# Sparse expert blocks brought back inside the last chunk, with their transfers on Pool's queue

## The chip, the core and the metric

The kernel runs on one core of a Trainium2 chip. The metric is the device time of one execution in microseconds. TensorE (PE in the profile) does matmuls, VectorE (DVE) and ScalarE (ACT) elementwise work, GpSimd (POOL) some of it and DMA issues, SyncE (SP) DMA issues. Each engine takes its instructions in the order in which they stand on its own queue, and waits on semaphores for the others.

## What is computed

One layer of a decoder: attention beside a state-space mixer, and then the PEER expert network, in which each token chooses 128 of 16384 experts (8 heads of 16). Only the second half matters here:

```python
    def block(args):
        hb, ib, gb = args
        u = jnp.take(u_experts, ib, axis=0)
        pre = jnp.einsum('thkd,td->thk', u, hb).astype(jnp.float32)
        act = (jax.nn.gelu(pre, approximate=False) * gb).astype(hb.dtype)
        vsel = jnp.take(v_experts, ib, axis=0)
        return jnp.einsum('thk,thkd->td', act, vsel)
...
        x = x + g2 * peer_ffn(h2, w_query[l], sub_keys[l], u_experts[l], v_experts[l])
```

512 tokens with 2048 features; the output is the residual stream after both halves.

## The kernel before

**Two ways for the experts.** Of the 512 tokens, 160 are *sparse*: their experts' rows are gathered one by one. The other 352 (TD) are *dense*: all 16384 experts are computed for them, and a matrix of gates, zero for the experts not chosen, picks. The dense part is the large one on TensorE, the sparse part lies beside it on VectorE and Pool.

**The dense loop** goes over 16 chunks of 8 expert blocks (`for c in range(P // CH)`). In a chunk, `up` makes eight blocks of activations (matmuls "up"), VectorE multiplies them with the gates gc, and they are split in a high and a low part, ah and al. Then four passes over dg follow, each for four of the 16 groups of 128 features: 96 matmuls "pv" (8 blocks, 4 features, 3 products of the split parts) fill four PSUM accumulators pv0 to pv3, and four VectorE instructions x1s add them to the residual stream (x1s <- pv, modT, x1s). In the last chunk each x1s is followed by a store of its 128 features of the dense tokens, issued on SP.

**Weights** come by SP in pieces of 512 KB (ur, vr), ScalarE rounds them to a high part (uh, vh), and VectorE makes the low part (ul, vl, line 131). These splits have to be ready ahead of TensorE.

**The sparse part** is a list of 320 entries, for each of 160 slots one u row and one v row per partition: Pool gathers 1 MB (`pick`, line 1080) into one of three buffers g. A u entry (line 1086) multiplies with the tokens and sums; a v entry (line 1098) adds a row times its coefficient to an accumulator with tokens on the partitions: acc0 for the first 128 slots (128 tokens), accx for the last 32 (32 tokens, four partitions to a token). `step()`, called 16 times a chunk, issues and consumes the entries; consumption is held two entries behind (AHEAD).

**The end.** After the loops the remaining entries are consumed, and each accumulator is brought back to features. ACT issues the load of the tokens' residual stream xb. TensorE turns the accumulator (lines 1178 and 1180): for acc0 16 transposes, for accx 16 matmuls with the stationary accx and the moving matrix `fold`, which also sums the four partitions of a token. VectorE adds the result to xb (line 1183), and SP issues the store. xb takes a buffer of the same three as g; the results "op" and the accumulators pv share 8 PSUM banks (`vps`).

**Order.** The program is written in the order of the loops, but a scheduler with a timeline model of its own puts the instructions of each engine into their final order; what stands on a queue is then fixed.

Of the kernel before, what the change touches and what calls it, by code (L numbers as in the profile page):

```python
# [11 lines left out]
F32 = mybir.dt.float32  # L12
# [5 lines left out]
ALU = mybir.AluOpType  # L18
# [4 lines left out]
P = 128  # L23
T = 512
D = 2048
KD = D // P
NT = T // P
EPS = 1e-6
CH = 8
# [3 lines left out]
NS = 160  # L33
XT = NS - P
XQ = P // XT
# [15 lines left out]
def layer(ctx, tc, xT, cols_d, pos_d, w_ada, w_in, w_kr, w_uq, w_ukv, w_out, w_q, subk, u_t, u_r, v_t, v_d, out):  # L51
    nc = tc.nc
# [49 lines left out]
    ident = cp.tile([P, P], F32, name="ident")  # L102
# [21 lines left out]
    SH1, SC1, G1, SH2, SC2, G2 = range(6)  # L124

    def mod(m, k):
        return modT[:, m * 16 + k:m * 16 + k + 1]
# [196 lines left out]
    for q in range(4):  # L324
        ada_pe(SC1, q)
        ada_pe(SH1, q, page_a)
        for k in range(4 * q, 4 * q + 4):
            hk = tp("hk")
            nc.scalar.activation(hk, xs[k], AF.Identity, scale=mod(SC1, k), bias=mod(SH1, k))
            a = [page_a("hh", F32R), page_a("hl", F32R)]  # L330
# [8 lines left out]
    for i in range(6):  # L339
        t = page_b("lat")  # L340
# [3 lines left out]
    ps = psum("pjk")  # L344
# [5 lines left out]
    ps = psum2("kdp")  # L350
# [100 lines left out]
    for n in (11, 9, 7, 5, 3, 1):  # L451
# [7 lines left out]
                                   op1=ALU.mult)  # L459
    cs = ep.tile([P, 64], F32, name="cs")  # L460
    ncs = ep.tile([P, 64], F32, name="ncs")
    ps = psum2("csp")
# [3 lines left out]
    ps = psum2("csl")  # L466
# [319 lines left out]
    x1 = []  # L786
    s2 = Sq("s2", nc.vector)
    for d in range(KD):
        t = page_b("x1")[:, :T]
        nc.sync.dma_start(t, x1d[d])  # L790
        ps = psum("wob")
# [274 lines left out]
    def gath(name):  # L1066
        return pe_.tile([P, D], F32, tag="gath", name=name, bufs=3)
# [45 lines left out]
    def step():  # L1113
        nonlocal issued, done, unit
        unit += 1
        goal = max(0, min(total, total * (unit - LAG) // (units * 15 // 16 - LAG)))
        while done < goal - AHEAD:
            f, s, _ = sparse[done]
            with tc.issue_after(pace[1].ins):
                f(s, fetched[done])  # L1120
            fetched[done] = None
            done += 1
        while issued < goal:
            f, s, table = sparse[issued]
            fetched.append(pick(s, table, "g"))
            issued += 1

    for c in range(P // CH):
        A = []
        for jj in range(CH):  # L1130
            j = c * CH + jj
            if j % GC == 0:
                gc = pe_.tile([P, NTG, GC, 32], F32, tag="gc", name="gc", bufs=1)
                nc.sync.dma_start(gc.rearrange("p g j t -> p g (j t)"), gd[j // GC])
            ge = ges.pop(j) if j in ges else up(j)
            g3 = ge.rearrange("p (g t) -> p g t", t=32)
            nc.vector.tensor_tensor(g3, g3, gc[:, :, j % GC, :], ALU.mult)
            a = [pp.tile([P, TD], F32R, tag=t, name=t) for t in ("ah", "al")]
            nc.scalar.activation(a[0], ge, AF.Copy)
            pace[1] = sub_lo(nc.vector, a[1], ge, a[0])  # L1140
            A.append(a)
            step()
        if c == 0:
            nc.gpsimd.dma_start(x1[:, CH:], x1d[CH:, :, NS:].rearrange("k p t -> p k t"))
        for dg in range(4):
            pv = [vps.tile([P, T], F32, tag="v", name=f"pv{i}") for i in range(4)]
            for j2 in range(CH // 2):
                vw = wload(v_d[c, dg, j2], (2, T), eng=nc.vector, name="v")
                pace[1] = pace[0]
                for q in range(2):  # L1150
                    jj = j2 * 2 + q
                    for dd in range(4):
                        mm(pv[dd][:, :TD], [w[:, q, dd * P:(dd + 1) * P] for w in vw], A[jj], jj == 0, jj == CH - 1)
                if j2 % 2:
                    step()
            for dd in range(4):
                d = dg * 4 + dd
                nc.vector.scalar_tensor_tensor(x1[:, d], pv[dd][:, :TD], mod(G2, d), x1[:, d], op0=ALU.mult, op1=ALU.add)
                if c == P // CH - 1:
                    nc.sync.dma_start(out[d][:, NS:], x1[:, d])  # L1160
    AHEAD = 0
    while done < total:
        step()

    fold = pe_.tile([P, XT], F32, name="fold", bufs=1)
    nc.vector.tensor_tensor(fold, ident[:, 0:XT], ident[:, XT:2 * XT], ALU.add)
    for q in range(2, XQ):
        nc.vector.tensor_tensor(fold, fold, ident[:, q * XT:(q + 1) * XT], ALU.add)
    for acc, t0, n in ((acc0, 0, P), (accx, P, XT)):
        xb = gath("xb")[:, :KD * n].rearrange("p (k t) -> p k t", k=KD)  # L1170
        nc.scalar.dma_start(xb, x1d[:, :, t0:t0 + n].rearrange("k p t -> p k t"))
        for q in range(4):
            ps = vps.tile([P, T], F32, tag="v", name="op")
            for j in range(4):
                d = q * 4 + j
                a, o = acc[:, d * P:(d + 1) * P], ps[:, j * P:j * P + n]
                if n == P:
                    nc.tensor.transpose(o, a, ident)
                else:
                    nc.tensor.matmul(o, a, fold, start=True, stop=True)  # L1180
            for j in range(4):
                d = q * 4 + j
                nc.vector.scalar_tensor_tensor(xb[:, d], ps[:, j * P:j * P + n], mod(G2, d), xb[:, d], op0=ALU.mult,
                                               op1=ALU.add)
        nc.sync.dma_start(out[:, :, t0:t0 + n].rearrange("k p t -> p k t"), xb)


def arrange(x, c, positions, w_ada, b_ada, w_in, q_a_norm, w_uq, kv_a_norm, w_ukv, q_norm, k_norm, attn_out_norm,
# [60 lines left out]
```

## Time and profile before

| | us |
|---|---|
| median of 3 runs | 3236.68 |
| lowest, highest run | 3230.98, 3237.19 |
| profiled execution, its time | 3230.25 |
| profiled execution, its span | 3228.5 |
| TensorE busy | 3063.2 (95%) |
| VectorE busy | 2488.2 (77%) |
| GpSimd busy | 941.4 (29%) |

The span goes from the first to the last instruction; the time has 1.75 us more around it. Busy time is the union of an engine's instructions, so an engine that is busy for a whole stretch sets that stretch's length, and one that is not may still be waited for at one place in it.

### The profile page before, as it was taken

The page shows a single profiled execution, that of the slowest core. Times are in us where ns is not written, and L with a number is a line of the kernel's source. Part 1 is how long each engine was busy: PE and PEld are TensorE (multiplying, and loading weights), DVE is VectorE, ACT ScalarE, POOL GpSimd, SP SyncE. Part 2 cuts the span into 40 slices and gives each one's busy share as a digit, 9 for nine tenths or more (in the row PEclk, how much of TensorE's full clock was granted, in tenths as well). Part 3 has the DMA queues.
Part 4 walks back from the last instruction along what each step waited for, and adds up shares of the span by engine and source line. Part 5 has one row for each costly group of instructions (what it writes and reads, how often), then busy time and mean ns, then how long its engine had stood idle before and what let it go on. Part 6 is the DMA issues. An engine that isn't in the chain of part 4 may idle for free.

```text
span 3228.5 us, 46353 instructions
## 1 busy us (share of the span) xinstructions
PE 3063.2 (95%) x17881; PEld 2794.6 (87%) x17881; DVE 2488.2 (77%) x3904; ACT 1146.5 (36%) x1754; POOL 941.4 (29%) x650
## 2 busy tenths in 40 slices
PE   5998889889989889999999999999999999999999
PEld 2476766567767788999999999999999999999999
DVE  3247777577759997659888888888888888888887
ACT  2243225442262257733333333333332333332332
POOL 1143333014435566533221121122222222121211
PEclk9999999999999999999999999999999999999999
DMA  9626762429642247769998999899998999999997
GB/s 320 243 93 217 235 212 95 135 99 311 230 136 76 84 125 209 232 216 369 341 343 331 338 342 330 336 341 332 336 336 331 341 338 334 340 336 336 336 343 260
DMA packets 286189, 858.79 MB, mean 266 GB/s; under 512 B 35888, under 2 KB 95424, under 8 KB 245008
## 3 DMA queue, kind: packets, MB, share of 16 engines
q1 hardware_dynamic: 181648, 483.53, 42.7%
q0 software_dynamic: 46448, 337.01, 28.0%
q10 hardware_dynamic: 57872, 35.30, 3.7%
q8 instruction: 140, 2.29, 0.3%
q14 instruction: 81, 0.66, 0.1%
HBM read 816.65 MB, written 39.06 MB: 265 GB/s over the span
## 4 chain that ended last, share of the span: by engine, by line
PE 61%; DVE 5%; ACT 2%; DMA 1%; issue 1%; POOL 1%; ACTq 0%; SPq 0%; POOLq 0%; DVEq 0%
PE pv L138 10%; PE pv L137 10%; PE pv L136 10%; PE up L136 9%; PE up L138 9%; PE up L137 9%; PE gps L1022 1%; ACT gt L1025 1%; DVE oj L1020 1%; DMA h2f<-h2b 0%; DMA sk<-subk 0%; PE wq L137 0%; PE wq L136 0%; DVE topi L933 0%; DVE topi L930 0%
## 5 line engine op out<-in xcount | busy, mean ns | idle before, releaser
L138 PE MATMUL up<-h2hi,ul 128*128 128x352 f32 x2048 | 664.2, 324 | 0.3 <-POOL ul L131 0.3
L136 PE MATMUL up<-h2hi,uh 128*128 128x352 f32 x2048 | 663.1, 324 | 0.0
L137 PE MATMUL up<-h2lo,uh 128*128 128x352 f32 x2048 | 661.2, 323 | 0.0
L136 PE MATMUL pv<-ah,vh 128*128 128x352 f32 x2048 | 659.3, 322 | 1.4 <-ACT ge L964 1.4
L137 PE MATMUL pv<-al,vh 128*128 128x352 f32 x2048 | 659.2, 322 | 0.0
L138 PE MATMUL pv<-ah,vl 128*128 128x352 f32 x2048 | 651.0, 322 | 0.0
L156 ACT ACTIVATE vh<-vr 128x1024 fp32r<-128x1024 f32 x256 | 272.1, 1063 | 624.8 <-PE pv L137 528.3
L156 ACT ACTIVATE uh<-ur 128x1024 fp32r<-128x1024 f32 x256 | 271.3, 1060 | 541.0 <-PE up L137 405.0
L131 DVE TENSOR_TENSOR vl<-vr,vh 128x1024 fp32r<-128x1024 f32 x256 | 312.6, 1223 | 157.4 <-ACT vh L156 157.1
L131 POOL TENSOR_TENSOR wl<-wr,wh 128x1024 fp32r<-128x1024 f32 (+2 forms) x134 | 294.7, 2204 | 465.8 <-ACT wh L156 377.4
L138 PEld LDWEIGHTS up<-h2hi,ul 128*128 128x128 f32 x2048 | 389.1, 190 | 0.7 <-POOL ul L131 0.7
L136 PEld LDWEIGHTS pv<-ah,vh 128*128 128x128 f32 x2048 | 384.6, 188 | 1.7 <-ACT ge L964 1.7
L137 PEld LDWEIGHTS up<-h2lo,uh 128*128 128x128 f32 x2048 | 385.9, 188 | 0.0
L136 PEld LDWEIGHTS up<-h2hi,uh 128*128 128x128 f32 x2048 | 385.8, 188 | 0.0
L137 PEld LDWEIGHTS pv<-al,vh 128*128 128x128 f32 x2048 | 384.6, 188 | 0.0
L138 PEld LDWEIGHTS pv<-ah,vl 128*128 128x128 f32 x2048 | 382.9, 188 | 0.0
L131 DVE TENSOR_TENSOR ul<-ur,uh 128x1024 fp32r<-128x1024 f32 x214 | 261.8, 1223 | 130.8 <-ACT uh L156 130.8
L1080 POOL DMA_INDIRECT g<-u_r,idx x128 | 163.2, 1275 | 576.3 <-DVE acc L1098 485.6
L1080 POOL DMA_INDIRECT g<-v_t,idx x128 | 155.7, 1217 | 541.1 <-DVE pre L1086 526.1
L1098 DVE SCALAR_TENSOR_TENSOR acc<-g,cf,acc 128x2048 f32<-128x2048 f32 x127 | 297.6, 2343 | 0.0
L1086 DVE CUSTOM_DVE_ANT_0 g<-g,h2t 128x2048 f32<-128x2048 f32 x128 | 292.0, 2283 | 2.1 <-DMA g<-u_r,idx 2.1
L269 DVE SCALAR_TENSOR_TENSOR acc<-wada,ca,acc 128x512 f32<-128x512 f32 x180 | 200.6, 1114 | 74.7 <-DMA wada<-w_ada 71.7
(465 smaller groups left out, 4786.8 us busy)
## 6 DMA issues: line engine op xcount, KB each, us to landing
ur<-u_t SPq DMA_DIRECT2D x256, 512.0 KB
vr<-v_d SPq DMA_DIRECT2D x256, 512.0 KB
wada<-w_ada SPq DMA_DIRECT2D x96, 512.0 KB
wada<-w_ada SPq DMA_DIRECT2D x128, 256.0 KB
gd<-gt ACTq DMA_DIRECT2D x22, 1024.0 KB
gc<-gd SPq DMA_DIRECT2D x32, 704.0 KB
wr<-w_in SPq DMA_DIRECT2D x40, 512.0 KB
wadq<-w_ada SPq DMA_DIRECT2D x32, 512.0 KB
```

Source lines behind the costliest of these rows:

```text
L131: return eng.tensor_tensor(lo, src, hi.bitcast(F32), ALU.subtract)
L136: nc.tensor.matmul(ps, a[0], b[0], start=start, stop=False)
L137: nc.tensor.matmul(ps, a[0], b[1], start=False, stop=False)
L138: pace[5] = nc.tensor.matmul(ps, a[1], b[0], start=False, stop=stop)
L156: nc.scalar.activation(hi[:, :n], raw[:, :n], AF.Copy)
L269: nc.vector.scalar_tensor_tensor(acc, wt[:, kk], ca[:, k:k + 1], acc, op0=ALU.mult, op1=ALU.add)
L1020: nc.vector.tensor_scalar(oj[:, t], iota, ijg[:, 1, t0 + t:t0 + t + 1], ijg[:, 2, t0 + t:t0 + t + 1], op0=ALU.is_equal, op1=ALU.mult)
L1022: pace[2] = nc.tensor.matmul(ps[:, t * P:(t + 1) * P], oi[:, t], oj[:, t], start=True, stop=True)
L1025: nc.scalar.activation(gt[:, :, t4_ * 4:t4_ * 4 + 4].rearrange("p j t -> p t j"), pv_[:, :, jh * 64:(jh + 1) * 64], AF.Copy)
L1080: nc.gpsimd.indirect_dma_start(out=g, out_offset=None, in_=table, in_offset=bass.IndirectOffsetOnAxis(ap=ix[:, s - s0:s - s0 + 1], axis=0))
L1086: nc.vector.tensor_tensor_reduce(g, g, rows, 1.0, 0.0, ALU.mult, ALU.add, accum_out=pre[:, s:s + 1])
L1098: nc.vector.scalar_tensor_tensor(acc, g, cf[:, s:s + 1], acc, op0=ALU.mult, op1=ALU.add)
```

## The change

The block that brings an accumulator back becomes a function `back`. It is called inside the last chunk: for acc0 behind the stores of the first pass (dg 0), for accx behind those of the second (dg 1). The load of xb and the store of the result are issued from Pool's queue (ACT and SP before), and so are the 16 stores of the dense tokens (SP before). When all gathers are issued, `step` consumes what is left at once, without the lag of two entries; the loop that did this behind the chunks is gone. `fold` is written ahead of the loop.

```diff
@@ step()
+        while issued == total and done < total:
+            f, s, _ = sparse[done]
+            f(s, fetched[done])
+            done += 1
+
+    fold = pe_.tile([P, XT], F32, name="fold", bufs=1)
...
+    def back(acc, t0, n):
+
+        xb = gath("xb")[:, :KD * n].rearrange("p (k t) -> p k t", k=KD)
+        nc.gpsimd.dma_start(xb, x1d[:, :, t0:t0 + n].rearrange("k p t -> p k t"))
+        for q in range(4):
+            ps = vps.tile([P, T], F32, tag="v", name="op")
+            for j in range(4):
+                d = q * 4 + j
+                a, o = acc[:, d * P:(d + 1) * P], ps[:, j * P:j * P + n]
+                if n == P:
+                    nc.tensor.transpose(o, a, ident)
+                else:
+                    nc.tensor.matmul(o, a, fold, start=True, stop=True)
+            for j in range(4):
+                d = q * 4 + j
+                nc.vector.scalar_tensor_tensor(xb[:, d], ps[:, j * P:j * P + n], mod(G2, d), xb[:, d], op0=ALU.mult,
+                                               op1=ALU.add)
+        nc.gpsimd.dma_start(out[:, :, t0:t0 + n].rearrange("k p t -> p k t"), xb)
...
                 if c == P // CH - 1:
-                    nc.sync.dma_start(out[d][:, NS:], x1[:, d])
-    AHEAD = 0
-    while done < total:
-        step()
-
-    fold = pe_.tile([P, XT], F32, name="fold", bufs=1)
...
-    for acc, t0, n in ((acc0, 0, P), (accx, P, XT)):
...
-        nc.scalar.dma_start(xb, x1d[:, :, t0:t0 + n].rearrange("k p t -> p k t"))
...
-        nc.sync.dma_start(out[:, :, t0:t0 + n].rearrange("k p t -> p k t"), xb)
+                    nc.gpsimd.dma_start(out[d][:, NS:], x1[:, d])
+            if c == P // CH - 1 and dg in (0, 1):
+                assert done == total
+                back(*((accx, P, XT) if dg else (acc0, 0, P)))
```

**TensorE's queue at the end of the program, before.** Behind the last pv matmul of the last pass stand the 16 transposes of acc0 and the 16 matmuls of accx with fold (the numbers name buffers):

```order
L137 MATMUL pv3_28662<-al_28260,vh_28755 128x352
L138 MATMUL pv3_28662<-ah_28259,vl_28756 128x352
L1178 MATMUL op_28799<-ident_83,acc0_9412 128x128 x4
L1178 MATMUL op_28808<-ident_83,acc0_9412 128x128 x4
L1178 MATMUL op_28817<-ident_83,acc0_9412 128x128 x4
L1178 MATMUL op_28826<-ident_83,acc0_9412 128x128 x4
L1180 MATMUL op_28838<-fold_28793,accx_9414 128x32 x4
L1180 MATMUL op_28847<-fold_28793,accx_9414 128x32 x4
```

TensorE's queue at the end of the second pass of the last chunk, after (pv3_28443 is the last accumulator of this pass, pv0_28611 the first of the third):

```order
L136 MATMUL pv3_28443<-ah_28265,vh_28536 128x352
L137 MATMUL pv3_28443<-al_28266,vh_28536 128x352
L138 MATMUL pv3_28443<-ah_28265,vl_28537 128x352
L1149 MATMUL op_28574<-fold_12266,accx_9414 128x32 x4
L1149 MATMUL op_28583<-fold_12266,accx_9414 128x32 x4
L1149 MATMUL op_28592<-fold_12266,accx_9414 128x32 x4
L1149 MATMUL op_28601<-fold_12266,accx_9414 128x32 x4
L136 MATMUL pv0_28611<-ah_27794,vh_28617 128x352
L137 MATMUL pv0_28611<-al_27795,vh_28617 128x352
L138 MATMUL pv0_28611<-ah_27794,vl_28618 128x352
```

The 16 matmuls that read accx moved from the end of the queue to a place ahead of the third pass; acc0's transposes likewise stand between the first and the second pass.

**VectorE's queue at the end of the program, before** (accx lines are additions of gathered rows, vl the weight splits, x1s and xb the additions to the residual stream):

```order
L131 TENSOR_TENSOR vl_28666<-vr_28663,vh_28665 128x1024
L1098 SCALAR_TENSOR_TENSOR accx_9414<-g_27651,cf_12265,accx_9414 128x2048
L131 TENSOR_TENSOR vl_28696<-vr_28693,vh_28695 128x1024
L1158 SCALAR_TENSOR_TENSOR x1s_7512<-pv0_28527,modT_107,x1s_7512 128x352
...
L131 TENSOR_TENSOR vl_28726<-vr_28723,vh_28725 128x1024
L131 TENSOR_TENSOR vl_28756<-vr_28753,vh_28755 128x1024
L1098 SCALAR_TENSOR_TENSOR accx_9414<-g_27715,cf_12265,accx_9414 128x2048
L1098 SCALAR_TENSOR_TENSOR accx_9414<-g_27717,cf_12265,accx_9414 128x2048
L1158 SCALAR_TENSOR_TENSOR x1s_7512<-pv0_28659,modT_107,x1s_7512 128x352
```

VectorE's queue from the second pass's last x1s on, after:

```order
L1186 SCALAR_TENSOR_TENSOR x1s_7512<-pv3_28443,modT_107,x1s_7512 128x352
L131 TENSOR_TENSOR vl_28678<-vr_28675,vh_28677 128x1024
L1098 SCALAR_TENSOR_TENSOR accx_9414<-g_27584,cf_12265,accx_9414 128x2048
L1098 SCALAR_TENSOR_TENSOR accx_9414<-g_27655,cf_12265,accx_9414 128x2048
L1098 SCALAR_TENSOR_TENSOR accx_9414<-g_27719,cf_12265,accx_9414 128x2048
L1098 SCALAR_TENSOR_TENSOR accx_9414<-g_27721,cf_12265,accx_9414 128x2048
L1152 SCALAR_TENSOR_TENSOR xb_28401<-op_28403,modT_107,xb_28401 128x128 x4
...
L1152 SCALAR_TENSOR_TENSOR xb_28572<-op_28601,modT_107,xb_28572 128x32 x4
L131 TENSOR_TENSOR vl_28708<-vr_28705,vh_28707 128x1024
```

The last additions into accx, spread over the third and fourth pass before, stand in one row behind the second pass's x1s; all 32 xb additions follow, ahead of the split for the third pass's last quarter.

**Pool's queue at the end of the program, after** (before, the gathers alone stand there):

```order
L1080 DMA g_27582<-v_t,idxx_9425 128x2048
L1188 DMA out<-x1s_7512 128x352 x4
L1080 DMA g_27584<-v_t,idxx_9425 128x2048
L1080 DMA g_27655<-v_t,idxx_9425 128x2048
L1080 DMA g_27719<-v_t,idxx_9425 128x2048
L1188 DMA out<-x1s_7512 128x352 x4
L1080 DMA g_27721<-v_t,idxx_9425 128x2048
L1140 DMA xb_28401<-x1d_3207 128x16x128
L1140 DMA xb_28572<-x1d_3207 128x16x32
L1154 DMA out<-xb_28401 128x16x128
L1154 DMA out<-xb_28572 128x16x32
L1188 DMA out<-x1s_7512 128x352 x8
```

The stores of the first and second pass stand between the last gathers, and the loads and stores of xb between them and the stores of the last two passes.

## Rows read from the trace of the kernel before

**Rows 1.** The page: span, busy time of engines, DMA share in 40 slices.

```profile
span 3228.5 us, 46353 instructions
...
PE 3063.2 (95%) x17881; PEld 2794.6 (87%) x17881; DVE 2488.2 (77%) x3904; ACT 1146.5 (36%) x1754; POOL 941.4 (29%) x650
...
DMA  9626762429642247769998999899998999999997
```

**Rows 2.** Busy time by stretch, last three passes; the columns are the first row.

```profile
core 0: us, PE busy (x) PEld busy (x) DVE busy (x) ACT busy (x) POOL busy (x), PEclk, DMA share, GB/s
3169.30:3184.70 15.40, 15.40 (x99) 15.40 (x98) 11.78 (x9) 4.25 (x4) 1.87 (x2) 1.00 1.02 384
3184.70:3200.00 15.30, 15.30 (x97) 15.30 (x97) 13.29 (x14) 4.25 (x4) 1.87 (x2) 1.00 0.88 311
3200.00:3215.30 15.30, 15.30 (x98) 15.30 (x97) 9.09 (x9) 2.12 (x2) 0.00 (x0) 1.00 0.40 106
```

**Rows 3.** Timeline, TensorE, end: start, us, instruction, form, count, [idle before <- releaser].

```profile
3215.34 1.91 PE L1178 MATMUL op<-ident,acc 128*128 128x128 f32 x16
3217.09 4.20 PE L1180 MATMUL op<-fold,accx 128*128 128x32 f32 x32
```

**Rows 4.** Timeline, VectorE, third pass to the end.

```profile
3193.47 1.22 DVE L131 TENSOR_TENSOR vl<-vr,vh 128x1024 fp32r<-128x1024 f32 x1 [0.35 <-ACT vh L156]
3194.61 2.34 DVE L1098 SCALAR_TENSOR_TENSOR accx<-g,cf,accx 128x2048 f32<-128x2048 f32 x1
...
3198.76 2.06 DVE L1158 SCALAR_TENSOR_TENSOR x1s<-pv,modT,x1s 128x352 f32<-128x352 f32 x4 [0.23 <-PE pv L138]
...
3206.16 4.73 DVE L1098 SCALAR_TENSOR_TENSOR accx<-g,cf,accx 128x2048 f32<-128x2048 f32 x2
3214.10 2.06 DVE L1158 SCALAR_TENSOR_TENSOR x1s<-pv,modT,x1s 128x352 f32<-128x352 f32 x4 [3.20 <-PE pv L138]
3216.07 6.75 DVE L1183 SCALAR_TENSOR_TENSOR xb<-op,modT,xb 128x128 f32<-128x128 f32 x32
```

**Rows 5.** Timeline, Pool: DMA issues in a row, a direct one, the last gather.

```profile
1359.77 0.94 POOL L1080 DMA_INDIRECT g<-u_r,idx  x1 [0.30 <-issue]
...
1379.35 0.97 POOL L1144 DMA_DIRECT2D x1s<-x1d  x1 [3.29 <-DVE al L131]
...
3193.39 0.94 POOL L1080 DMA_INDIRECT g<-v_t,idxx  x1 [5.26 <-DVE accx L1098]
```

**Rows 6.** Timeline, Pool and VectorE: gathers that somebody waited for.

```profile
1547.70 1.74 POOL L1080 DMA_INDIRECT g<-v_t,idx  x1 [4.46 <-DVE pre L1086]
...
1555.76 1.68 POOL L1080 DMA_INDIRECT g<-v_t,idx  x1 [3.23 <-DMA g<-v_t,idx]
...
2482.01 3.88 POOL L1080 DMA_INDIRECT g<-u_r,idx  x1 [5.24 <-DVE acc L1098]
...
2494.86 2.29 DVE L1086 CUSTOM_DVE_ANT_0 g<-g,h2t 128x2048 f32<-128x2048 f32 x1 [1.91 <-DMA g<-u_r,idx]
```

**Rows 7.** op alone by stretch: us, PE, PEld, DVE busy, PEclk, DMA share, GB/s.

```profile
3217.20:3219.20 2.00, 2.00 (x21) 2.00 (x19) 2.00 (x9) 1.00 0.21 72
3220.20:3221.20 1.00, 1.00 (x6) 0.95 (x5) 1.00 (x8) 0.50 0.00 0
```

**Rows 8.** Timeline, TensorE, restart after idle time.

```profile
908.01 1.22 PE L136 MATMUL wq<-h2h,wh 128*128 128x512 f32 x2 [3.48 <-ACT h2h L820]
...
912.01 0.63 PE L138 MATMUL wq<-h2h,wl 128*128 128x512 f32 x1
...
912.75 0.39 PE L137 MATMUL wq<-h2l,wh 128*128 128x512 f32 x1
```

**Rows 9.** The last stores: SP's issues of x1s, and stretches as in rows 2.

```profile
3214.71 1.81 SPq L1160 DMA_DIRECT2D out<-x1s  x4
...
3218.00:3219.00 1.00, 1.00 (x11) 1.00 (x11) 1.00 (x5) 0.00 (x0) 0.00 (x0) 1.00 0.03 8
...
3227.30:3228.50 1.20, 0.00 (x0) 0.00 (x0) 0.00 (x0) 0.00 (x0) 0.00 (x0) 0.50 0.00 0
```

More of the change, by code (lines that the diff above doesn't have):

```diff
@@ L1126, in step @@
             issued += 1
+        while issued == total and done < total:
[3 more added lines that the diff above has]
+    fold = pe_.tile([P, XT], F32, name="fold", bufs=1)
+    nc.vector.tensor_tensor(fold, ident[:, 0:XT], ident[:, XT:2 * XT], ALU.add)
+    for q in range(2, XQ):
+        nc.vector.tensor_tensor(fold, fold, ident[:, q * XT:(q + 1) * XT], ALU.add)
+    def back(acc, t0, n):
[15 more added lines that the diff above has]
+        nc.gpsimd.dma_start(out[:, :, t0:t0 + n].rearrange("k p t -> p k t"), xb)
     for c in range(P // CH):
@@ L1159, in layer @@
                 if c == P // CH - 1:
-                    nc.sync.dma_start(out[d][:, NS:], x1[:, d])
-    AHEAD = 0
-    while done < total:
-        step()
-    fold = pe_.tile([P, XT], F32, name="fold", bufs=1)
-    nc.vector.tensor_tensor(fold, ident[:, 0:XT], ident[:, XT:2 * XT], ALU.add)
-    for q in range(2, XQ):
-        nc.vector.tensor_tensor(fold, fold, ident[:, q * XT:(q + 1) * XT], ALU.add)
-    for acc, t0, n in ((acc0, 0, P), (accx, P, XT)):
-        xb = gath("xb")[:, :KD * n].rearrange("p (k t) -> p k t", k=KD)
-        nc.scalar.dma_start(xb, x1d[:, :, t0:t0 + n].rearrange("k p t -> p k t"))
[L1172 to L1184, printed above, removed]
-        nc.sync.dma_start(out[:, :, t0:t0 + n].rearrange("k p t -> p k t"), xb)
+                    nc.gpsimd.dma_start(out[d][:, NS:], x1[:, d])
+            if c == P // CH - 1 and dg in (0, 1):
+                assert done == total
+                back(*((accx, P, XT) if dg else (acc0, 0, P)))
 def arrange(x, c, positions, w_ada, b_ada, w_in, q_a_norm, w_uq, kv_a_norm, w_ukv, q_norm, k_norm, attn_out_norm,
```

## Prediction

> **What bounds the kernel now.** The page comes first: TensorE is busy 95% of a span of 3228.5 us, VectorE 77%, GpSimd 29% [rows 1]. An average over stages doesn't say what a change at the end is worth, so the second view is the busy time over the last passes. A *pass* is one turn of the dg loop, 96 pv matmuls; the four of the last chunk I call dg0 to dg3. In dg1, dg2 and dg3 TensorE is busy 15.3 of 15.3 us at the full clock [rows 2], so every instruction put between those passes, and every wait of TensorE there, lengthens the run by its whole size. The same view shows DMA share falling from 1.02 to 0.40 and VectorE from 13.3 to 9.1 us towards the end.
>
> The third view is the end itself. The last pv matmul gives way to the op matmuls at 3215.34 [rows 3], the span ends at 3228.5: a tail of 13.2 us, of which TensorE works 6. A pass takes 15.33 us (x1s starts at 3198.76 and 3214.10 [rows 4]), so dg1 ends at 3184.7. The change shortens the tail and puts its work between the passes. The question is what the passes pay.
>
> **The change, part by part.** E is the end of dg1's matmuls in the changed kernel.
>
> *acc0's block, between dg0 and dg1.* 16 transposes, 3215.34 to 3217.09 today [rows 3]: +1.75 us, all on the path. acc0 is complete long before (the last 32 slots go to accx), so nothing is waited for. dg1's accumulators reuse dg0's banks now, but x1s empties the first bank while the transposes run; cover: about 1.7 us of them against a first x1s of 0.58 us, and uncovered it would cost about 0.6.
>
> *accx's block, between dg1 and dg2.* Here lies the loss. TensorE takes its queue in order, and the fold matmuls read accx, so TensorE stands still until the last of the four remaining additions into accx is done. On VectorE these four stand behind dg1's four x1s and one weight split vl. x1s needs dg1's finished sums, and ends 0.8 us behind the last pv matmul (3216.16 against 3215.34 [rows 3, 4]). The split takes 1.14 us from start to start (3193.47 to 3194.61). Two additions in a row take 4.73 us, so 2.37 each [rows 4]. With all rows of the table at hand the last addition ends at E + 0.8 + 1.14 + 4 x 2.37 = E + 11.4. That is the floor of the wait, made only of VectorE's own durations.
>
> Rows are not all at hand. Three buffers hold gathered rows, so the fourth gather waits for the first addition (E + 4.3), and on Pool's queue it stands behind dg1's four stores. A DMA issue on Pool takes 0.94 to 0.97 us with 0.30 between two [rows 5], 1.25 in all; the first store can go at E - 0.6, so the gather starts at E + 4.4. How long a gather takes shows where somebody waited for one: 1547.70 to 1555.76, 8.1 us, and 2482.01 to 2494.86, 12.9 us [rows 6]. The floor from below is 4.65 us, at which it hides behind the two additions in between. Both waits fell in slices in which the DMA engines were busy 0.8 to 0.9 [rows 1]; here the weight stream stops with TensorE, though stores of dg1 lie ahead on the same queue. I take the middle of 4.65 and 8.1, 6.4 us: landed at E + 10.8, added by E + 13.2. **Wait of TensorE: 13.2 us**, bounds 11.4 and 19.7 (with 12.9).
>
> The Trainium skill ("DMA: Bandwidth & Descriptors", section "Anatomy of one DMA — SWDGE (gpsimd) path") fits a DMA from Pool at 2.0 us plus its bytes over 436 GB/s; for the 1 MB of a gather my estimate by it is 4.4 us, the gather would hide, and the sum below would be 1.8 us smaller. The rows above are nearly twice that under load, so I don't take it.
>
> Then the fold matmuls: 32 in 4.20 us [rows 3], of which most ran at the full clock (21 in 2.0 us) and the last at half (6 in 1.0 us, one begun before) [rows 7]. That is 3.6 us for 32 at the full clock and 6.4 at half. Earlier TensorE restarted at 908.01 after 3.48 us of idle time and ran slow until past 912.01, a 512-column matmul taking 0.63 us; at 912.75 it takes 0.39 [rows 8], so about 4.4 us went by at half. After 13 us of idle I take half: **+6.4**, bounds 3.6 and 6.4. Since the clock fell in today's tail while TensorE ran nothing but such small matmuls (1.00, then 0.50 [rows 7]), I take it that they don't bring it back, and that dg2's first 4.4 us run at half speed: **+2.2**, bounds 0 and 2.2.
>
> A second gate stands beside this one: dg2's four accumulators sit in the banks of acc0's block, which are empty when xb has been added, and xb's load is issued by Pool behind the fourth gather, at about E + 6.8. With 8.1 us for its 1 MB it lands at E + 14.9. The 32 xb additions take 6.75 us today [rows 4], so these 16, the larger ones, about 4: the first bank is free at E + 16, the last at E + 19. TensorE comes there at E + 19.6, so I cost it at nothing; the cover is about 3.6 us, and a load as slow as 12.9 us would cost 1.1. The xb additions also stand ahead of the split that dg2's last quarter needs, 11.5 us into the pass: they are done by E + 23, it is needed at E + 31. Free, with 8 us to spare.
>
> *The tail.* Behind dg3 only x1s and four stores remain. x1s ends 0.8 us after the last matmul. Four Pool issues at 1.25 us begin 0.6 us before it, so the fourth begins 3.15 us after. On SP the fourth store was issued at 3216.2 (start of the group 3214.71, 1.81 us for four) and the traffic has ceased by about 3218; from the last traffic (3227.3) to the span's end it is 1.2 us [rows 9]. With 0.6 more for the longer issue that is 2.4 for landing and 1.2 to close: 6.8 us in place of 13.2. **-6.4**, bounds -8.6 (issues as fast as x1s delivers) and -3.4 (issues of 1.7 us, a length that gathers show too [rows 6]).
>
> *At no cost.* The stores of dg0 hold Pool for 5 us, from its first x1s (3198.76 less two passes, so 3168.1, and 0.58) to 3173.7. The gather behind them can't start sooner anyway: its buffer comes free by an addition that stands behind the x1s and a split, at 3168.1 + 2.06 + 1.14 + 2.37 = 3173.7. Uncovered they would delay an addition that is wanted 10 us later. SP loses the stores, so its weight loads no longer stand behind them: TensorE never waits for a weight in these passes [rows 2], so that is worth nothing. Flushing the last entries without the two-entry lag moves no engine's instructions before the last chunk. ACT loses two issues of 0.37 us, hidden beside TensorE.
>
> *Sum:* 1.75 + 13.2 + 6.4 + 2.2 - 6.4 = **+17.2 us**. The profiled execution took 3230.25 us (span 3228.5, 1.75 around it), so it would be 3247.5. It is the lowest of the times shown; the median of the three runs is 3236.68 and stands 6.4 above it, so I add to the median: 3253.9. All floors together give 1.75 + 11.4 + 3.6 + 0 - 8.6 = +8.2, all ceilings 1.75 + 19.7 + 6.4 + 2.2 - 3.4 = +26.7.
>
> **Rivals.**
>
> *The block fits better than I think.* Gather hidden, clock kept up, stores at x1s's pace: the floors, +8.2 us, 3244.9. For it: DMA is lighter late in dg2 and dg3 than before. Against it: at this place the last of them all need to go well at once.
>
> *Pool is held up.* Issues of gathers took up to 3.88 us beside VectorE's work instead of 0.94 [rows 6]. In this place a slow issue delays the gather by 2.9 us, and the four stores of the tail by 0.75 each, 3.0: 17.2 + 5.9 = +23.1, 3259.8. Against it: the issues late in the trace are 0.94 [rows 5], and the additions that run beside these are of the same kind. The Trainium skill ("SBUF — State Buffer", in its warning on the "DVE blocks DMA" trap) says that descriptors of Pool's DMAs can't be written while VectorE holds the port shared with GpSimd, and names SP's or ACT's queues as the way out; by it moving the stores to Pool would cost as in this rival.
>
> *Not slower.* One mechanism would do it: the four additions run ahead, during dg1, so that accx is complete when TensorE arrives and only the shorter tail is left: 1.75 + 3.6 - 8.6 = -3.2 us, 3233.5. It decides at a wait of 3.2 us: below it the tail pays for everything. Against it: VectorE's queue has x1s of dg1 and a split ahead of them, and 4 x 2.37 alone is 9.5 us. It needs the built order not to be the order that runs; for the kernel before, order and trace agree row by row at this place [rows 4].
>
> *It doesn't do what it says.* For accx's block that is the forecast itself: it lies inside the chunk, but bare, because nothing runs beside it on TensorE.
>
> **How the numbers follow.** A difference of 0.2%, 6.5 us, is about what a measurement of this kernel can tell from none. Forecast 0.73; better fit 0.14; Pool held up 0.10; not slower 0.03. Of the better fit a third falls within 0.2% (the runs before lie 6 us apart), as does most of the last: slower 0.91, same 0.07, faster 0.02. The range takes in the better fit and the slow Pool, but not all bounds at once: from +11 on the lowest run shown (3231.0) to +24 on the highest (3237.2), 3242 to 3261.
>
> **What the profile of the changed kernel would show.** TensorE idle once in the last chunk, 11 to 15 us, ended by VectorE's last accx addition, and clock at half behind it; four additions in a row on VectorE with a gap ahead of the fourth, ended by the gather; 16 transposes of 1.75 us between dg0 and dg1 with no wait; Pool's last stores about 1.25 us apart; span's end 6 to 8 us behind the last pv matmul. I would be wrong if TensorE went on into dg2 with no idle time of 10 us, if the additions were spread over dg1, or if the tail stayed at 13 us.

## The result, and the profile after

| | us |
|---|---|
| before, median of 4 runs | 3234.07 (3230.98 to 3237.19) |
| changed, median of 4 runs | 3253.38 (3251.07 to 3254.89) |
| ratio | 1.0063, 95% interval 1.0050 to 1.0075 |
| changed, profiled execution and its span | 3254.89, 3253.2 |

The changed kernel is slower by 19.3 us, 0.6%. The forecast was +17.2 us, 3253.9. That 3253.9 lies within 0.6 us of the measured time is partly luck: the forecast added its 17.2 to a median of 3236.68 over three runs, and over four runs that median is 3234.07.

The two profiled spans differ by 24.7 us, but dg0's first x1s starts at 3172.58 in the changed kernel and at 3168.1 in the one before, ahead of anything that the change can hold up. In the runs below that point lies between 3166.9 and 3176.7, whatever the kernel. So for the last chunk I use one measure throughout, the **last stretch**: from dg0's first x1s to the end of the span. Before it is 60.4 us (3168.10 to 3228.5), after the change 80.6 (3172.58 to 3253.2): +20.2 us.

The page of the changed kernel, its span and the busy time of the engines, as in [rows 1]:

```profile
span 3253.2 us, 46343 instructions
...
PE 3069.7 (94%) x17881; PEld 2801.6 (86%) x17881; DVE 2490.8 (77%) x3904; ACT 1147.2 (35%) x1754; POOL 959.1 (29%) x670
```

The shares look like those of before: 20 us in 3253 don't show in an average. The stretches of the last chunk do, with the columns of [rows 2]: TensorE's wait, the fold matmuls, the start of dg2, most of the rest of it, and the tail.

```profile
core 0: us, PE busy (x) PEld busy (x) DVE busy (x) ACT busy (x) POOL busy (x), PEclk, DMA share, GB/s
3190.80:3207.40 16.60, 0.28 (x2) 0.00 (x0) 11.11 (x7) 1.06 (x1) 7.34 (x7) 0.61 0.96 317
3207.50:3214.60 7.10, 6.78 (x32) 6.78 (x32) 5.86 (x27) 0.00 (x0) 1.07 (x1) 0.50 0.11 24
3214.70:3217.90 3.20, 3.20 (x12) 3.20 (x13) 1.07 (x7) 0.00 (x0) 1.16 (x1) 0.50 0.80 230
3218.00:3230.40 12.40, 12.40 (x78) 12.40 (x78) 3.68 (x3) 3.18 (x3) 0.00 (x0) 0.99 0.23 46
3246.90:3253.20 6.30, 0.32 (x3) 0.04 (x1) 0.98 (x2) 0.00 (x0) 1.95 (x4) 0.93 0.32 116
```

In the first stretch TensorE does next to nothing while VectorE works 11.1 of 16.6 us and DMA is at 0.96. In the second and third the granted clock is 0.50, the lower level of 1.2 GHz. TensorE's own timeline gives the terms (start, us, form, and in brackets the idle time with what ended it; what stood at the end of [rows 3] stands here in the middle):

```profile
3173.82 1.91 PE L1147 MATMUL op<-ident,acc 128*128 128x128 f32 x16
...
3190.76 0.32 PE L138 MATMUL pv<-ah,vl 128*128 128x352 f32 x1
3207.82 7.03 PE L1149 MATMUL op<-fold,accx 128*128 128x32 f32 x32 [16.75 <-DVE accx L1098]
3214.67 0.64 PE L136 MATMUL pv<-ah,vh 128*128 128x352 f32 x1
...
3217.75 0.49 PE L137 MATMUL pv<-al,vh 128*128 128x352 f32 x1
3218.04 0.42 PE L138 MATMUL pv<-ah,vl 128*128 128x352 f32 x1
3218.30 0.32 PE L136 MATMUL pv<-ah,vh 128*128 128x352 f32 x1
```

One wait of 16.75 us, ended by VectorE's last addition into accx; 32 fold matmuls in 6.85 us (3207.82 to 3214.67); then dg2's first 12 matmuls 0.29 us apart in place of 0.16. VectorE's rows in that wait, and Pool's with the gathers and stores:

```profile
3189.68 2.06 DVE L1186 SCALAR_TENSOR_TENSOR x1s<-pv,modT,x1s 128x352 f32<-128x352 f32 x4 [0.23 <-PE pv L138]
3192.05 1.23 DVE L131 TENSOR_TENSOR vl<-vr,vh 128x1024 fp32r<-128x1024 f32 x1 [0.31 <-ACT vh L156]
3193.19 4.73 DVE L1098 SCALAR_TENSOR_TENSOR accx<-g,cf,accx 128x2048 f32<-128x2048 f32 x2
3199.07 2.35 DVE L1098 SCALAR_TENSOR_TENSOR accx<-g,cf,accx 128x2048 f32<-128x2048 f32 x1 [1.15 <-DMA g<-v_t,idxx]
3205.42 2.35 DVE L1098 SCALAR_TENSOR_TENSOR accx<-g,cf,accx 128x2048 f32<-128x2048 f32 x1 [4.00 <-DMA g<-v_t,idxx]
3209.01 6.76 DVE L1152 SCALAR_TENSOR_TENSOR xb<-op,modT,xb 128x128 f32<-128x128 f32 x32 [1.24 <-DMA xb<-x1d]
```

```profile
3188.45 1.80 POOL L1080 DMA_INDIRECT g<-v_t,idxx  x1 [5.48 <-DVE accx L1098]
3190.56 2.21 POOL L1188 DMA_DIRECT2D out<-x1s  x4 [0.30 <-DVE x1s L1186]
3195.81 2.99 POOL L1080 DMA_INDIRECT g<-v_t,idxx  x1 [3.04 <-DVE accx L1098]
3198.79 1.22 POOL L1140 DMA_DIRECT2D xb<-x1d  x1
...
3246.70 1.60 POOL L1188 DMA_DIRECT2D out<-x1s  x3 [13.16 <-DVE x1s L1186]
3248.53 0.54 POOL L1188 DMA_DIRECT2D out<-x1s  x1 [0.23 <-issue]
```

Split, then four additions, as foretold; but the third waits 1.15 us for its rows and the fourth 4.00. dg1's four stores take Pool 2.2 us, not 5 (dg0's took 4.6, from 3173.46 to 3178.09, with 2.4 us of waiting in the middle). The fourth gather is not held by them (Pool is idle from 3192.77 on, the buffer comes free at 3195.5); its issue takes 2.99 us, and it ends at 3198.80, 0.9 us behind VectorE's second addition. Its rows land at 3205.42, 9.6 us after the issue began. The third's late rows cost nothing by themselves: without that 1.15 us VectorE would have stood as much longer in front of the fourth.

### The profile page after: what moved, and what is told of

The parts are those of the page before. It is cut to its first block, busy times and chain, and to the rows that moved or that the text cites. A ratio compares the mean times of both kernels' runs of the same rounds, so it can differ in the third digit from the quotient of the medians.

```text
span 3253.2 us, 46343 instructions
## 1 busy us (share of the span) xinstructions
PE 3069.7 (94%) x17881; PEld 2801.6 (86%) x17881; DVE 2490.8 (77%) x3904; ACT 1147.2 (35%) x1754; POOL 959.1 (29%) x670
## 4 chain that ended last, share of the span: by engine, by line
PE 61%; DVE 5%; ACT 2%; DMA 2%; issue 1%; POOL 1%; ACTq 0%; SPq 0%; POOLq 0%; DVEq 0%
PE pv L136 10%; PE pv L137 10%; PE pv L138 10%; PE up L138 9%; PE up L136 9%; PE up L137 9%; PE gps L1022 1%; ACT gt L1025 1%; DVE oj L1020 1%; PE wq L137 1%; PE wq L136 1%; PE wq L138 0%; DMA h2f<-h2b 0%; DMA sk<-subk 0%; DVE topi L933 0%
```

## The experiments

The theory after the result: the loss is TensorE's wait for accx's last four additions, with the half clock that it brings, and the queues are a side matter. The main rival: Pool's queue is what costs. The verdicts rest on the time against the kernel before on the same chip (its medians were 3232.4 to 3233.0 there, and 3234.07 beside the changed kernel), on the last stretch, and on its last part, from dg3's first x1s to the end (14.4 us before, 7.4 after the change).

| kernel | median, us | against before | ratio, 95% interval | last stretch | last part |
|---|---|---|---|---|---|
| changed | 3253.38 | +19.3 | 1.0050 to 1.0075 | 80.6 (+20.2) | 7.4 |
| e1, accx at the end | 3232.99 | +0.5 | 0.9999 to 1.0017 | 61.5 (+1.1) | 12.1 |
| e2, queues of before | 3248.81 | +16.3 | 1.0046 to 1.0072 | 79.7 (+19.3) | 5.3 |
| e3, queues alone | 3232.76 | -0.2 | 0.9991 to 1.0009 | 62.7 (+2.3) | 16.7 |
| e6, four additions out | 3229.51 | -3.0 | 0.9981 to 1.0002 | 60.1 (-0.3) | 7.2 |
| e7, additions halved | 3253.63 | +21.1 | 1.0058 to 1.0087 | 78.7 (+18.3) | 7.3 |
| e8p, accx behind dg2 | 3241.71 | +8.7 | 1.0021 to 1.0040 | 69.7 (+9.3) | 7.3 |
| e9p, accx in dg3 | 3234.47 | +1.5 | 0.9989 to 1.0013 | 61.8 (+1.4) | 7.4 |
| e9s, the same, SP and ACT | 3228.89 | -4.1 | 0.9978 to 0.9996 | 58.8 (-1.6) | 5.8 |
| e10s, one addition later | 3228.63 | -3.8 | 0.9972 to 0.9993 | 58.2 (-2.2) | (moved) |
| e11, stores on SP | 3249.02 | +16.6 | 1.0030 to 1.0064 | 76.5 (+16.1) | 5.0 |

Times and last stretches agree within 3 us; the rest is the drift between executions ahead of the last chunk.

**One half undone each.** e1 keeps Pool's queues and puts accx's block back at the end:

```diff
-            if c == P // CH - 1 and dg in (0, 1):
+            if c == P // CH - 1 and dg == 0:
...
+    back(accx, P, XT)
```

> The changed kernel with one part undone: acc0's block stays behind dg0 and all its loads and stores stay on Pool's queue, but accx's block goes back behind the last pass. Theory (the loss is TensorE's wait for the last accx addition, and the half clock behind it): no idle time of TensorE at the end of dg1, full clock in dg2, and a tail of about 10 us (the changed kernel 6.1, the kernel before 13.2). Against the kernel before +1.75 for the transposes and about -3 in the tail: 3229 to 3236 us where the kernel before has 3234, so some 19 us under the changed kernel. Rival (Pool's queue is what costs, by gathers held behind stores and by slow issues): it stays near the changed kernel, above 3245 us.

e2 keeps the places and undoes the queues (`nc.gpsimd.dma_start` of xb back to `nc.scalar`, of both stores to `nc.sync`):

> The changed kernel with the other part undone: both blocks stay where the change put them, but xb is loaded from ACT's queue and everything is stored from SP's, as before. The order of the computing instructions is the same. Theory (place of accx's block costs, the queue hardly): the four stores held Pool only 2.2 us, until 3192.8, and the fourth gather was released at 3194 or later, so TensorE's wait stays at 15 to 17 us and the time within 2 us of the changed kernel: 3251 to 3255 us. The gather's issue on Pool stays near 3 us, since VectorE's additions run beside it as before. Rival (Pool's queue delays the fourth gather, or the xb load behind it sets the end of the wait): wait 11 to 13 us, time 3246 to 3250 us.

e1 came out at 3232.99, no wait at the end of dg1: the loss is gone (TensorE waits 1.3 us for x1s at the start of dg3 instead). e2's time, 3248.81, lies outside the theory's range and where the rival put it, but the rival's mechanism didn't happen: the wait grew.

```profile
3190.64 2.93 POOL L1080 DMA_INDIRECT g<-v_t,idxx  x1 [4.94 <-DVE accx L1098]
3201.87 2.35 DVE L1098 SCALAR_TENSOR_TENSOR accx<-g,cf,accx 128x2048 f32<-128x2048 f32 x1 [6.06 <-DMA g<-v_t,idxx]
3204.27 7.04 PE L1149 MATMUL op<-fold,accx 128*128 128x32 f32 x32 [18.36 <-DVE accx L1098]
```

These are e2's fourth gather, the addition that waits for it, and TensorE at the place of the 16.75. In e2 the fourth gather landed 11.2 us after its issue began (3190.64 to 3201.87), with the 1 MB load of xb running beside it from ACT's queue, against 9.6 in the changed kernel. What made up for it is the last part, 5.3 us where Pool's stores take 7.4.

**Without the last four additions.** e6 leaves four entries out (`sparse = sparse[:-4]`), everything else stays.

> The changed kernel without the last four entries of the list of gathered rows of v: four gathers and four additions into accx less, all else in its place and on its queue. Leaves out a part of the sum in accx. Theory (the wait is for those four additions): accx is complete before TensorE arrives, the wait at the end of dg1 falls from 16.75 us to under 4, and so does the half clock behind it; 1.75 for the transposes, about 3.6 for the fold matmuls at the full clock and -7 in the tail give -2 against the kernel before: 3230 to 3236 us. Rival (the second gate, xb's load and its additions that free the banks for dg2, is as late as the additions): TensorE is held in front of dg2 instead, by 5 us or more, and the time is 3240 us or more.

It took 3229.51, a little under its range. The fold matmuls follow the pv matmuls of dg1 with no wait; so xb's load, the second gate, holds nobody here. (It goes out 20 us earlier in e6, with no gather ahead of it; but in the changed kernel too TensorE goes from the fold matmuls to dg2 without a wait.) Stretches of e6, columns as above: the fold matmuls, what follows, and the rest of dg2:

```profile
3184.90:3188.60 3.70, 3.70 (x36) 3.70 (x34) 3.39 (x9) 1.06 (x1) 2.15 (x4) 1.00 0.92 334
3188.90:3192.20 3.30, 3.30 (x13) 3.30 (x14) 3.30 (x15) 0.00 (x0) 0.20 (x1) 0.54 0.43 150
3192.30:3204.00 11.70, 11.70 (x74) 11.70 (x74) 5.36 (x16) 3.19 (x3) 2.04 (x2) 0.99 0.47 114
```

Without idle time the fold matmuls run at the full clock (32 in 3.6 us), but right behind them the clock is at half for 3.4 us all the same, 1.6 us lost. So without any wait the change would be worth 1.75 + 3.6 + 1.6 - 7.2 = -0.3 us: that, and not the -6.4 of the tail, is what there was to win at this place and with these queues. The 1.6 is this execution's; such a dip doesn't come in all of the kernels below.

**The price of the gathers.** e7 cuts each of the last four additions into two halves of 1024 columns, to let Pool in between them.

```diff
-            nc.vector.scalar_tensor_tensor(acc, g, cf[:, s:s + 1], acc, op0=ALU.mult, op1=ALU.add)
+            for h in ([slice(0, D // 2), slice(D // 2, D)] if s >= NS - 4 else [slice(0, D)]):
+                nc.vector.scalar_tensor_tensor(acc[:, h], g[:, h], cf[:, s:s + 1], acc[:, h], op0=ALU.mult, op1=ALU.add)
```

> The changed kernel with the last four additions into accx cut into two instructions of 1024 columns each. In the changed kernel the issue of the fourth gather on Pool took 2.99 us and ended 0.9 us behind VectorE's second addition. Theory (VectorE's addition holds Pool's issue up until it is finished): with an end of an instruction every 1.2 us, the fourth gather's issue takes 1.8 us or less, its rows land about 1 us earlier, TensorE's wait falls to about 15.5 us plus up to 0.4 for the four more instructions, and the time is 0.5 to 1.2 us under the changed kernel. Rival (the issue is long for a cause of its own): it stays at 3.0 us, and the time is the same or 0.4 us longer.

e11 is the changed kernel with the stores of the dense tokens back on SP (`nc.sync.dma_start(out[d][:, NS:], x1[:, d])`), xb still on Pool.

> The changed kernel with the stores of the dense tokens back on SP's queue; xb stays on Pool's, and both blocks where the change put them. In the changed kernel TensorE waited 16.75 us, with both queue changes undone 18.4, while xb's load ran from ACT's queue beside the fourth gather; from dg3's first x1s to the end it took 7.4 and 5.3 us. Theory (Pool's stores cost nothing ahead of the gather; xb's load beside the gather is what made the wait longer with both undone; stores from SP land sooner): wait 15.5 to 17 us, last part 5.3 to 5.8 us, so 1 to 3 us under the changed kernel, +16 to +19 us against the kernel before: 3249 to 3252 us. Rival (the stores moved off Pool let the fourth gather go sooner): wait below 14 us, 3247 us or less. Rival (the wait of 18.4 had nothing to do with xb's load): it stays at 18 us or more.

Pool's fourth gather, VectorE's addition behind it and TensorE in e7:

```profile
3194.53 1.80 POOL L1080 DMA_INDIRECT g<-v_t,idxx  x1 [3.15 <-DVE accx L1099]
```

```profile
3203.28 2.48 DVE L1099 SCALAR_TENSOR_TENSOR accx<-g,cf,accx 128x1024 f32<-128x1024 f32 x2 [3.16 <-DMA g<-v_t,idxx]
```

```profile
3204.62 7.03 PE L1150 MATMUL op<-fold,accx 128*128 128x32 f32 x32 [14.95 <-DVE accx L1099]
```

The issue fell from 2.99 to 1.80 us, as the theory said, and the rows landed 8.75 us after its start in place of 9.6. VectorE's addition does hold Pool's issue. The wait fell by 1.8 us, but only 1.0 of it (idle 4.15 instead of 5.15 on VectorE, with the 0.99 ahead of the third addition) is the gathers'; the rest I had not planned: TensorE starts at 3204.6, behind the first half of the last addition (3203.28 plus 1.24), because the first fold matmuls read the first columns. In the time none of this shows: 1.0073 against 1.0063, with overlapping intervals. Here only the trace decides.

e11's fourth gather, the 1.13 and 2.55 us for which VectorE waited for the third and fourth, and TensorE:

```profile
3193.15 2.93 POOL L1080 DMA_INDIRECT g<-v_t,idxx  x1 [4.94 <-DVE accx L1098]
```

```profile
3196.40 2.35 DVE L1098 SCALAR_TENSOR_TENSOR accx<-g,cf,accx 128x2048 f32<-128x2048 f32 x1 [1.13 <-DMA g<-v_t,idxx]
3201.30 2.35 DVE L1098 SCALAR_TENSOR_TENSOR accx<-g,cf,accx 128x2048 f32<-128x2048 f32 x1 [2.55 <-DMA g<-v_t,idxx]
```

```profile
3203.71 7.04 PE L1149 MATMUL op<-fold,accx 128*128 128x32 f32 x32 [15.28 <-DVE accx L1098]
```

With these the wait can be taken apart. Wait less VectorE's idle time for gathers: changed kernel 16.75 - 5.15 = 11.60; e11 15.28 - 3.68 = 11.60; e2 18.36 - 6.76 (0.70 and 6.06) = 11.60. The wait is 11.6 us of VectorE's own work and whatever the gathers are late. Along the chain that ends it, the fourth gather is released 4.7 us into the wait in all three, takes 8.2, 9.6 and 11.2 us from its issue to its rows, and 2.4 us to be added: the three waits differ by this one gather. The issue of the fourth gather is as long in all three (2.93 to 2.99); from its end to the landing it takes 5.2 us in e11, 6.6 in the changed kernel, where the four stores go ahead of it on the same queue, and 8.3 in e2, beside xb's load. e11's 3249.02 lies at the low end of the theory's range, its wait and its last part of 5.0 just below theirs; neither rival came. One part of the theory failed: Pool's stores ahead of the gather weren't free, by the 1.4 us between 6.6 and 5.2. Each of these durations is from one execution.

**Moving the block on.** e8p puts accx's block behind dg2 (`dg in (0, 2)`), e9p inside dg3 behind its second weight piece:

```diff
+                if c == P // CH - 1 and dg == 3 and j2 == 1:
+                    back(accx, P, XT)
...
-            if c == P // CH - 1 and dg in (0, 1):
+            if c == P // CH - 1 and dg == 0:
```

> The changed kernel with accx's block one pass later, behind dg2; queues as in the changed kernel. One addition into accx instead of four stands behind dg2's x1s and a weight split. Theory (wait = x1s tail 0.8 + split 1.14 + 2.37 for each addition, while the rows are at hand): TensorE waits 4.3 us behind dg2, up to 1.5 more if a bank has to be emptied of acc0's transposes first; with 1.75, 3.6 to 6.4 for the fold matmuls, 0 to 2 at half clock and -7.2 in the tail: +2 to +9 against the kernel before, 3235 to 3242 us. Rival (the wait is set by the gather, whatever the number of additions): it stays above 10 us, 3246 us or more.

> The changed kernel with accx's block moved on, from behind dg1 to the inside of dg3 (behind its second weight piece), all queues as in the changed kernel. Theory (the block costs only where TensorE has to wait for accx): the four additions are spread over dg2 and dg3 again and done before TensorE comes to the fold matmuls, so no wait above 1 us; 1.75 for the transposes and 3.6 for the fold matmuls at the full clock are paid, up to 1.6 for a dip of the clock behind them, and the tail gives back 7.2 (14.4 to 7.2 us from dg3's first x1s to the end, as in the kernel without the last four entries): -2 to 0 us against the kernel before, 3229 to 3235 us. Rival (what is put inside a pass costs more than it saves in the tail, by weight splits and x1s held up behind the xb additions on VectorE): 3238 us or more, with TensorE waiting for vl or x1s in dg3.

TensorE in e8p, with one addition left behind the pass:

```profile
3206.37 7.04 PE L1149 MATMUL op<-fold,accx 128*128 128x32 f32 x32 [6.04 <-DVE accx L1098]
```

The wait is 6.04 us; the 1.7 above the 4.3 come from x1s, which start 0.9 us behind dg2's last matmul where they otherwise start 1.1 ahead of it (3189.68 against 3190.76 above): another addition stands in front of them (3198.61 to 3200.95). The time is at the upper end of what was expected. In e9p the wait for accx is gone, 3234.47 us: no better than before, where 0 to 2 us better was expected, since three small things use the gain up, 1.3 us of waiting for x1s at the start of dg3 (again that addition), 3.4 us at half clock from the last fold matmuls on, much as in e6, and Pool's tail. e9s is e9p with the queues of before:

> The same, with xb loaded from ACT's queue and everything stored from SP's. Theory (the queue is no matter): the same time within 3 us, 3228 to 3236 us, tail from dg3's first x1s to the end 6.5 to 8 us. Rival (Pool's queue shortens the tail, or lengthens it by issues held up): the tail differs by 2 us or more from that with Pool's queue.

> The kernel with accx's block inside dg3 and the queues of before, a second time, to see whether its gain of 4 us on the kernel before (ratio 0.9987) holds. Theory (less than 2 us of it are in the last chunk: 58.8 us from dg0's first x1s to the end against 60.4): ratio 0.998 to 1.000, 3228 to 3233 us. Rival (the gain was drift between runs): ratio 1.000 or more.

3228.89 and 3228.79 us, ratios 0.9987 and 0.9989; the interval of the second, 0.9978 to 1.0001, takes in 1. The last part is 5.8 us, 1.5 less than on Pool: between the two expectations. No dip of the clock followed the fold matmuls here, though they stand at the same place as in e9p, with 18 pv matmuls behind them in both traces. e9p first, then e9s:

```profile
3216.48 3.93 PE L1149 MATMUL op<-fold,accx 128*128 128x32 f32 x32
3220.22 0.64 PE L136 MATMUL pv<-ah,vh 128*128 128x352 f32 x1
3220.66 0.49 PE L137 MATMUL pv<-al,vh 128*128 128x352 f32 x1
```

```profile
3219.27 3.65 PE L1149 MATMUL op<-fold,accx 128*128 128x32 f32 x32
3222.76 0.41 PE L136 MATMUL pv<-ah,vh 128*128 128x352 f32 x1
3223.01 0.32 PE L137 MATMUL pv<-al,vh 128*128 128x352 f32 x1
```

Nor did it in e10s. e10s puts the addition that ran ahead of x1s behind them:

```diff
-        while issued == total and done < total:
+        while issued == total and done < total - KEEP:
...
+            if c == P // CH - 1 and dg == 2:
+                KEEP = 0
+                pace[1] = xs
+                step()
```

(KEEP starts at 2, xs is the last x1s of the pass, and each of these additions is issued behind pace[1].)

> The kernel with accx's block inside dg3 and the queues of before, with the addition into accx that stands ahead of dg2's x1s on VectorE put behind them. There TensorE waited 1.3 us at the start of dg3 for x1s, since that addition came first. Theory (TensorE waits there only for x1s): the 1.3 us go; the fold matmuls move later by 2.4 us of additions, so that some of xb's additions fall behind dg3's x1s and the last part grows by 0 to 1.5 us: -1.3 to +0.3 against the kernel with the block in dg3 and the queues of before, that is 3226 to 3231 us. Rival (the addition behind x1s makes TensorE wait in front of the fold matmuls by more than it saves): a wait of 2 us or more there, 3231 us or more.

TensorE waits for nothing in e10s's last chunk, and the last stretch is 58.2 us, the shortest, 0.5 under e9s's, of the 1.3 that the wait took. The time, 3228.63 us, 0.9983 (0.9972 to 0.9993), can't be told from e9s's. Of its 3.8 us against the kernel before 2.2 are seen in the last chunk; where the rest is from I can't say.

**The queues alone.** e3 is the kernel before with Pool's queue for xb and all stores.

> The kernel before with nothing but the queues changed: xb is loaded, and all is stored, from Pool's queue; both blocks stay at the end. Theory (queues carry no time): within 3 us of the kernel before, 3229 to 3236 us, tail 12 to 14 us from the last pv matmul to the end. Rival (Pool's queue costs, by gathers behind stores): TensorE waits for VectorE in the last chunk and the time is 3238 us or more.

No TensorE wait, and 3232.76 us: no difference that its interval of +-0.1% could tell. Its tail is longer, though: 15.4 us from the last pv matmul to the end, outside the 12 to 14 expected. The last stores of before, on SP, and of e3, on Pool:

```profile
3220.32 2.92 SPq L1185 DMA_DIRECT2D out<-xb  x2
```

```profile
3220.62 1.17 POOL L1185 DMA_DIRECT2D out<-xb  x1 [3.45 <-DVE xb L1183]
3223.16 1.16 POOL L1185 DMA_DIRECT2D out<-xb  x1 [1.36 <-DVE xb L1183]
```

VectorE ends at 3222.8 and 3222.9. SP's last issue is over at 3223.24 and the span ends 5.3 us later; Pool's at 3224.32 and 6.5 us later.

## Why the prediction was right

The direction, the place and the mechanism were those of the forecast, and the sum came within 3 us. Its terms, forecast and measured in the last stretch:

| term | forecast | measured |
|---|---|---|
| acc0's transposes | +1.75 | +1.75 (a pass took 17.10 us from x1s to x1s, 15.33 before) |
| wait for accx | +13.2 (11.4 to 19.7) | +16.75 |
| fold matmuls | +6.4 (3.6 to 6.4) | +6.85 |
| dg2's start at half clock | +2.2 (0 to 2.2) | +1.6 (12 matmuls 0.13 us longer) |
| tail | -6.4 (-8.6 to -3.4) | -7.0 |
| sum | +17.2 | +20.0 (last stretch +20.2, time +19.3) |

- **The floor of the wait** was right: 11.4 from VectorE's durations of [rows 3, 4], 11.6 measured three times over; 0.3 of it is the split waiting for ACT's vh, which I left out.
- **The gather** is the mis-sized term. I let only the fourth be late, by 1.8 us; the third and fourth were, by 1.15 and 4.00. The step that failed is the value between 4.65 and 8.1 us for a gather: the 13.2 was 4.4 us to the fourth gather's start, 6.4 for it and 2.4 for its addition, and these came out at 4.7, 9.6 and 2.4. The 9.6 is more than the row of 8.1 [rows 6], and not unusual: over all 320 gathers of this trace it takes 5.4 to 14.6 us from issue to landing, with a median of 8.8. I went below the row because the weight stream stops with TensorE; the DMA engines were busy 0.96 of the wait all the same (first stretch above). Two parts of the 9.6 were shown: the issue is held up beside VectorE (2.99 us; 1.80 with halved additions), and the stores ahead of it on the queue, the stores of x1s, cost 1.4 us of transfer (6.6, and 5.2 in e11). I had argued from [rows 5] that issues this late take 0.94; the late one of those rows, at 3193.39, began 0.08 us ahead of VectorE's next instruction, the split of [rows 4] at 3193.47.
- The rival **Pool is held up** was therefore half true: the issue was as long as it said (2.99 against up to 3.88), but the four stores of the tail were not held. The warning of the Trainium skill ("SBUF — State Buffer", the "DVE blocks DMA" trap) has Pool's descriptors held up while VectorE works, and the gathers' issues look like it: 2.99 us beside whole additions, 1.80 beside halved ones. But it ties this to a 2-port mode of VectorE, and no row tells whether these additions use one: that this is the cause isn't shown. It doesn't explain the tail, where VectorE runs no additions into accx.
- The estimate that I set aside, 4.4 us for a gather by the Trainium skill ("DMA: Bandwidth & Descriptors", "Anatomy of one DMA — SWDGE (gpsimd) path"), was rightly set aside: 8.2 to 11.2 us from the issue's start in these runs.
- **Pool's store issues** were mis-sized the other way: 0.55 us apart (four in 2.2), not 1.25. The tail, counted from 3247.06 (0.16 us behind the start of the last pv matmul, as the 3215.34 of the kernel before is), is 6.1 us, not 6.8. That fast issues still lose to SP's is the part I missed: the last part is 5.0 to 5.8 us with stores on SP (e2, e9s, e11) and 7.2 to 7.4 on Pool (changed, e6 to e9p).
- **The second gate** held nobody, but its cover was not what I said: xb's load landed 18 us behind dg1's end, not 14.9 (issue 3198.79, additions 3209.01), and TensorE came 24 us behind it only because its own wait was longer too; at the 19.6 of the forecast there would have been little cover or none.
- **No cost** for dg0's stores was right: they held Pool for 4.6 us, about the 5 of the forecast, though by a wait in their middle and not by slow issues; the gather behind them (issue 3178.71) was released by an addition, and in the changed kernel TensorE waits for nothing else in the last chunk.
- **Not slower** needed the additions to run ahead; e6 and e9s show what it would have given, -0.3 and -1.6 us in the last stretch, not the -3.2 that I worked out: in e6 because of the clock's dip and Pool's tail, in e9s mostly because of the 1.3 us for which dg3 waits for x1s. The 3.6 in that sum doesn't follow from 21 matmuls in 2.0 us as it is written (that gives 3.0 for 32), but e6 measured it.

## What to carry to other kernels

Work that is moved from the tail into the middle of a busy engine's queue is not removed: it saves only what hung on it at the end (7.0 us here) and costs its own time (5.4 us at the full clock) plus every wait for its operands, so look first at what must still be finished ahead of it on the other engines. Add up the durations of those pieces in order: the floor of 11.4 us alone decided this case; one pass later, with one addition left, the wait was 6.0, and in dg3 nothing. Where buffers are few, price a gather from the moment that its buffer comes free, and by rows in which the same neighbours run on VectorE, in the queue and on the DMA engines.

## What the runs showed of the hardware

- In the last chunk of these runs an indirect gather's issue on Pool took 0.94 to 1.01 us where Pool began it ahead of VectorE's next instruction, and 0.94 beside an x1s (e2 and e11, in dg1); 1.68 to 1.81 beside a weight split or a halved addition; 2.93 to 2.99 where it was released into the second of two additions of 128x2048. These longer ones ended 0.8 to 0.9 us behind the instruction beside them.
- The clock fell to half for 3.4 us right behind 32 fold matmuls with no idle time ahead of them (e6, e9p); in e9s, with these matmuls at the same place as in e9p, and in e10s it didn't until the tail. In the tail the kernel before took 4.20 us for the 32, the last of them at half, and e3 3.66. What decides this stays open.
- After 16.75 us of idle time the fold matmuls ran at half throughout, and the full clock came back 3.3 us after the pv matmuls began (3214.67 to about 3218.0).
- Direct stores of 176 KB took 2.2 us for four issues in a row on Pool and 1.8 to 2.0 on SP, and the end came 4.0 to 4.1 us after Pool's last issue and 2.6 to 3.3 after SP's (e2, e9s, e11). Why is open.
